# Gated channels one step ahead, four convolution taps a slot, and the context's part of queries and keys first: a change to the first layer of a two-layer trunk

## The chip, the cores and the metric

One core of a Trainium2 chip runs the whole program in one launch. The metric is device time in microseconds; the time before is 1056.01 us, the median of 3 runs (1055.93 to 1057.12). All data is float32. Products are made by TensorE (PE) out of high and low parts: a weight and its rounded copy, and the remainder.

## The reference, cut to what matters

Two layers work on 256 latent tokens (4 rows of 64) and 256 context tokens, 1024 channels wide. In the first layer both streams go through everything; the part that matters here is the token-mixing half:

```
p = h @ w_in[l]                      # columns: GLU | q k v | gates
u = a * sigmoid(g)                   # conv branch: 512 gated channels
u = dwconv1d(u, dw, dw_b)            # depthwise, 31 taps
u = silu(layernorm(u, ln_g, ln_b)) @ w_conv_out
q = rope_2d(q, ...); k = rope_2d(k, ...)           # latent tokens only
s_win = q . k_window * scale + bias; s_ctx = q . k_ctx * scale
p = softmax(concat([s_win, s_ctx]))  # latent queries: window keys and all context keys
y_attn = p_win . v_win + p_ctx . v_ctx             # context queries: context keys only
x = x + g1 * ((sig(gate0) * y_conv + sig(gate1) * y_attn) @ w_out)
```

After it come a gated MLP, and the same again in the second layer.

## The kernel before

**Products.** Activations lie with channels on the partitions. `group` (L201) makes one 128-channel tile of an input projection for 512 tokens (latent and context): 8 channel blocks by 3 matmuls (L197 to L199), 24 matmuls of 128x512, into one of four PSUM banks (tag `main`). Its weights come as one 512 KB tile, `raw`, fetched on SP's queue; ACT rounds it (`whi`, L216) and negates it (`wlo`, L217), and a DMA of POOL's queue (L218) adds `raw` to `wlo`. There are four buffers each of `raw`, `whi` and `wlo`, so that a `whi` is written when PE has done with the one four tiles earlier.

**Slots.** In the middle and at the end of each such group the program passes a `slot()` (L92): each generator in the list `side` goes on by one step. One is the convolution (`conv_run`, L677), which at each slot issues `rate` taps. Another is the attention (`att.run`, L452). The instructions are then put in order for each engine by a scheduler; each engine works its queue in that order.

**Convolution.** `glu(j)` (L687) makes a tile `u` of 128 gated channels out of two groups (ACT takes the gate's tanh, L691; DVE multiplies, L693), and appends 31 taps. A tap is one DVE instruction on 128x512 that adds into the tile `cb` (L671 the first, L673 the other 30). Four tiles make 124 taps. What is left of them when the attention is over is issued by `layer_norm` (L938) with 5 a slot; its sum over the four tiles (L949 to L951) goes to PE in a matmul (L955), after gate group 9.

**Queries and keys.** `qk(j)` (L843), for each of four pairs of heads, makes a group of queries and one of keys. On DVE the latent half is rotated: a product (L859), a shuffle (L860), a product (L861) and a sum (L864 for queries, L869 for keys). Then queries and keys are split into a high part on ACT (L881) and a low part on DVE (L882): the context half in one piece, the latent half of queries in one, that of keys in two of 128x160. In the code these pieces stand after the rotation; keys take the pieces in the order context, first window part, second window part.

**Attention.** `Attention.step` (L457) issues the scores of a pair (L495: 24 matmuls of 64 partitions, of both query tiles and both heads), the softmax (DVE bias and maximum L516, ACT exponential L519, DVE reciprocal L521, ACT scaling L522), the turning of the probabilities on PE (L561, copies on ACT L564) and the products with values (L578, L587). Context queries are done for two pairs at a time (L530 to L540, L567). `ahead(j)` makes steps at once until pair j has been issued.

**The order in the first layer.** The value projection and the first gated tile run first (to 56 us). Then follow `qk(0)`, and for j = 1 to 3 `glu_groups(j)` and `qk(j)`. `rate` is 2.0, and 3 from the end of the first turn of that loop. While the attention has work, up to five gate groups follow (`gate`, L708), and when it is over its memory goes to new tiles, into which modulation rows are loaded (L282, L154) for dot products on DVE (L304). There are 16 gate groups. The values of the window keys go through 16 small DMAs on SP's queue (L728).

Of the kernel before, what the change touches and what calls it, by code (L numbers as in the profile page):

```python
# [19 lines left out]
S = 256  # L20
GW = 64
# [32 lines left out]
def trunk(ctx: ExitStack, tc: tile.TileContext, xt, cvec, crow, wall, wada, params, bias_t, rope_t, out):  # L54
# [13 lines left out]
    def nm(s):  # L68
        uid[0] += 1
        return f"{s}_{uid[0]}"  # L70
# [561 lines left out]
    for l in range(DEPTH):  # L632
# [5 lines left out]
        with ExitStack() if last else start as e1a:  # L638
# [62 lines left out]
            def glu_groups(j):  # L701
                pa = in_group(T_GLU + 2 * (j - 1), ALL)
                pg = in_group(T_GLU + 2 * (j - 1) + 1, ALL)
                copied = None if last else att.ahead(j - 2)
                with tc.issue_after(copied.ins) if copied else ExitStack():
                    glu(j, pa, pg)

# [5 lines left out]
            with ExitStack() as e1b:  # L713
# [126 lines left out]
                rate[0] = 3 if last else 2.0  # L840
                add_side(conv)

                def qk(j):  # L843

                    att.ahead(j - 2)
                    bt = eb.tile([P, 5, NS_ // 2], F32, tag="bias", bufs=2 if last else 1, name=nm("bias"))
                    both = []
                    for what in range(2):
                        w = T if what == 0 else 2 * S
                        sc = HD ** -0.5 if what == 0 else 1.0  # L850
                        ps = in_group((T_Q, T_K)[what] + j, slice(0, w))
                        if what == 0:
                            with tc.issue_after(lastdma[0].ins):
                                sp.dma_start(bt, bias_t[l, j])
                        r1, r2 = tmp(), tmp()
                        got = back(ps[:, :w])
                        lat, ctx_ = (got[:, 0], got[:, 1]) if w > S else (got, None)
                        part = halves if w == S else lambda a: a
                        dve.tensor_tensor(part(r1[:, LAT]), lat, part(rope[:, 0, :]), ALU.mult)  # L859
                        dve.stream_shuffle(part(r2[:, LAT]), lat, SWAP16)  # L860
                        dve.tensor_tensor(r2[:, LAT], r2[:, LAT], rope[:, 1, :], ALU.mult)  # L861
# [8 lines left out]
                        f = eb.tile([P, 2, KN if what else w], F32R, tag="qk"[what], bufs=2, name=nm("qk"))  # L870
                        if what == 0:
                            to = [([f[:, a, LAT] for a in range(2)], rq[:, LAT])]
                            if T > S:
                                to.append(([f[:, a, CTX] for a in range(2)], ctx_))
                        else:
                            rv_ = r1[:, LAT].rearrange("p (r c) -> p r c", r=ROWS)
                            to = [([f[:, a, KCTX] for a in range(2)], ctx_)]
                            for d, c in ((slice(0, KL), slice(GW - TC, GW)), (slice(KX, KN), slice(0, TC))):
                                to.append(([f[:, a, d].rearrange("p (c r) -> p r c", r=ROWS) for a in range(2)], rv_[:, :, c]))
                        for (hi, lo), src in to:  # L880
                            act.activation(hi, src, AF.Identity, scale=sc)  # L881
                            end = dve.scalar_tensor_tensor(lo, src, sc, hi.bitcast(F32), ALU.mult, ALU.subtract)  # L882
                        both.append(f)
                    att.pair(j, *both, bt, end)

                if l == 0:
                    for t in range(4):
                        keep_v(t, pv[t])
                    qk(0)
                    arun = att.run()  # L890
                    add_side(arun)
                    for j in range(1, 4):
                        glu_groups(j)
                        qk(j)
                        rate[0] = 3
                else:
                    glu_groups(2)
                    rate[0] = 3
# [12 lines left out]
                n = 0  # L911
                if last:
                    add_side(arun)
                    for j in range(1, 4):
                        gate(ea, n)
                        n += 1
                        qk(j)
                while att.busy() and n < (14 if last else 5):
                    gate(ea, n)
                    n += 1  # L920
                while att.busy():
# [435 lines left out]
```

## Time and profile before

| | |
|---|---|
| median of 3 runs | 1056.01 us |
| the profiled execution, its own time | 1054.58 us |
| its span | 1052.8 us |
| mean granted TensorE clock | 0.997 |
| PE busy | 1032.4 us (98%) |
| DVE busy | 893.2 us (85%) |
| ACT busy | 565.6 us (54%) |
| first PE matmul of the stage of pairs and gated tiles | 56.20 us |
| matmul of the normalization's sum, L955 | 213.02 us |

A row of the timeline gives the start in the span, the length, engine, line, operation and tile, the count where rows are merged, and in square brackets how long the engine was idle before and who released it. A matmul of 128x512 is shown 0.38 us long, and the next begins 0.216 us later: PE is pipelined, so starts are what counts. The same holds on DVE, where a tap is shown 0.74 to 0.77 us long and the next instruction begins earlier. The waits view sums such idle time by the waiting and the releasing line. The windows view gives, for each stretch, its length, the busy time of the engines with the number of their instructions, the granted clock, the share of the DMA engines and GB/s.

### The profile page before, as it was taken

What the parts mean: (1) busy time and instruction counts of PE and PEld (TensorE: products, weight loads), DVE (VectorE), ACT (ScalarE), POOL (GpSimd) and SP (SyncE); (2) the same over time, 40 slices, a digit from 0 to 9 for tenths busy, and PEclk for the clock granted to TensorE, in tenths of its full rate; (3) what the DMA queues carried; (4) which work ended last, traced back from release to release, by engine and by line L of the source; (5) the groups of instructions that cost most, each with busy time, mean ns of one, the idle gap of its engine ahead of it and who ended that gap; (6) DMA issues with size and microseconds to landing.
All of it is one profiled execution on the core that took longest, in us unless ns stands there. A gap on an engine that the chain in (4) does not pass through costs nothing.

```text
span 1052.8 us, 17991 instructions
## 1 busy us (share of the span) xinstructions
PE 1032.4 (98%) x6886; PEld 932.9 (89%) x6886; DVE 893.2 (85%) x1608; ACT 565.6 (54%) x921; POOL 43.7 (4%) x59
## 2 busy tenths in 40 slices
PE   9999999999999999999999999999999999999997
PEld 7787788888889988888888889999889999999996
DVE  6568899999998787878788888799899988988883
ACT  4458768545434644444444223545777666766652
POOL 1111110011000000000000000000000000000000
PEclk9999999999999999999999999999999999999998
DMA  9989674888945345454545887556734485666781
GB/s 374 305 221 229 156 181 121 258 255 236 305 146 177 104 140 160 140 164 143 166 145 160 301 289 249 180 189 209 208 123 135 161 292 176 193 201 199 221 283 57
DMA packets 59511, 209.26 MB, mean 199 GB/s; under 512 B 7201, under 2 KB 7457, under 8 KB 59425
## 3 DMA queue, kind: packets, MB, share of 16 engines
q1 hardware_dynamic: 54384, 190.77, 55.3%
q0 software_dynamic: 4752, 17.30, 8.7%
q8 instruction: 54, 0.88, 0.3%
q14 instruction: 33, 0.26, 0.1%
q10 hardware_dynamic: 288, 0.04, 0.0%
HBM read 187.63 MB, written 1.05 MB: 179 GB/s over the span
## 4 chain that ended last, share of the span: by engine, by line
PE 68%; DVE 17%; ACT 5%; DMA 4%; issue 3%; SPq 1%; DVEq 0%; ACTq 0%
PE main L197 20%; PE main L198 20%; PE main L199 20%; DVE cb L673 6%; PE main L736 4%; DVE wlo L168 3%; DMA raw<-in_wall 2%; DVE t L304 2%; DMA own<-in_wada 1%; SPq L728 1%; PE sc L197 1%; PE sc L199 1%; PE sc L198 1%; DVE qk L882 1%; ACT pp L519 1%
## 5 line engine op out<-in xcount | busy, mean ns | idle before, releaser
L197 PE MATMUL main<-h,whi 128*128 128x256 f32 (+1 forms) x1328 | 433.1, 326 | 1.2 <-DVE qk L882 1.2
L198 PE MATMUL main<-h,whi 128*128 128x256 f32 (+1 forms) x1328 | 430.2, 324 | 0.9 <-DVE h L1001 0.7
L199 PE MATMUL main<-h,wlo 128*128 128x256 f32 (+1 forms) x1328 | 429.9, 324 | 1.2 <-DVE wlo L168 1.1
L167 ACT CAST whi<-raw 128x1024 fp32r<-128x1024 f32 (+1 forms) x211 | 218.3, 1039 | 234.8 <-PE main L198 173.6
L168 DVE TENSOR_TENSOR wlo<-raw,whi 128x1024 fp32r<-128x1024 f32 (+1 forms) x211 | 253.6, 1208 | 67.2 <-ACT whi L167 66.4
L197 PEld LDWEIGHTS main<-h,whi 128*128 128x128 f32 x1328 | 252.8, 190 | 22.0 <-issue 1.3
L199 PEld LDWEIGHTS main<-h,wlo 128*128 128x128 f32 x1328 | 252.5, 190 | 18.5 <-DVE wlo L168 1.8
L198 PEld LDWEIGHTS main<-h,whi 128*128 128x128 f32 x1328 | 252.7, 190 | 18.3 <-DVE h L1001 1.0
L304 DVE CUSTOM_DVE_ANT_0 t<-own,sb,par 128x1024 bf16<-128x1024 f32 x120 | 151.8, 1282 | 6.8 <-DMA own<-in_wada 6.8
L673 DVE SCALAR_TENSOR_TENSOR cb<-u,par,cb 128x512 f32<-128x512 f32 (+1 forms) x240 | 144.7, 620 | 2.8
L198 PE MATMUL main<-fl,whi 128*128 128x256 f32 (+1 forms) x396 | 122.8, 310 | 0.0
L197 PE MATMUL main<-fh,whi 128*128 128x256 f32 (+1 forms) x396 | 122.8, 310 | 0.0
L199 PE MATMUL main<-fh,wlo 128*128 128x256 f32 (+1 forms) x396 | 122.5, 310 | 0.0
L197 PEld LDWEIGHTS main<-fh,whi 128*128 128x128 f32 x396 | 75.6, 191 | 3.8 <-ACT fh L1095 0.2
L198 PEld LDWEIGHTS main<-fl,whi 128*128 128x128 f32 x396 | 75.6, 191 | 3.7 <-DVE fl L1096 0.2
L199 PEld LDWEIGHTS main<-fh,wlo 128*128 128x128 f32 x396 | 75.5, 191 | 3.6
L216 ACT CAST whi<-raw 128x1024 fp32r<-128x1024 f32 x33 | 34.6, 1049 | 36.0 <-PE main L198 30.5
L404 ACT ACTIVATE h<-t,mod 128x256 fp32r<-128x256 f32 x56 | 25.2, 503 | 34.8 <-DVE t L403 34.3
L218 POOL DMA_DIRECT2D wlo<-raw x33 | 28.9, 877 | 258.9 <-ACT wlo L217 107.6
L736 PE MATMUL main<-whi,h 128*128 128x512 f32 x128 | 38.5, 386 | 0.2
L1105 ACT ACTIVATE t<-t 128x512 f32<-128x512 f32 x22 | 13.9, 632 | 41.3 <-DVE t L1074 41.3
L217 ACT ACTIVATE wlo<-whi 128x1024 fp32r<-128x1024 f32 x33 | 35.0, 1061 | 0.5
(214 smaller groups left out, 1268.8 us busy)
## 6 DMA issues: line engine op xcount, KB each, us to landing
raw<-in_wall SPq DMA_DIRECT2D x240, 512.0 KB, 4.3
own<-in_wada SPq DMA_DIRECT2D x72, 512.0 KB, 4.7
wlo<-raw POOLq DMA_DIRECT2D x33, 512.0 KB, 5.4
raw<-in_wada SPq DMA_DIRECT2D x16, 512.0 KB, 5.8
bias<-in_bias_t SPq DMA_DIRECT2D x8, 520.0 KB, 5.3
row<-in_wada SPq DMA_DIRECT2D x8, 512.0 KB, 5.1
sb<-in_crow SPq DMA_DIRECT2D x5, 512.0 KB, 4.8
x<-in_xt SPq DMA_DIRECT2D x4, 512.0 KB, 5.1
```

The source lines that it names most:

```text
L167: act.copy(hi[:, c], r[:, c])
L168: dve.tensor_tensor(lo[:, c], r[:, c], hi[:, c].bitcast(F32), ALU.subtract)
L197: pe.matmul(ps, w[0], order(xh), start=start, stop=False)
L198: pe.matmul(ps, w[0], order(xl), start=False, stop=False)
L199: pe.matmul(ps, w[1], order(xh), start=False, stop=stop)
L216: act.copy(hi, r)
L217: act.mul(lo, hi.bitcast(F32), -1.0)
L218: pool.dma_start(lo, r, accum_op=ALU.add)
L304: dve.tensor_tensor_reduce(tmp().bitcast(BF16), r, v, 1.0, pr(l, BADA + n, 1), ALU.mult, ALU.add, mods[l][:, n, s : s + 1])
L404: high = act.activation(hi[:, c], y[:, c], AF.Identity, bias=b)
L673: dve.scalar_tensor_tensor(cb[j], src, w, cb[j], ALU.mult, ALU.add)
L736: mm = pe.matmul(pv[t], h1[n == 1][k][:, c], runs(w[n == 2][:, b]), start=k + n == 0, stop=k == KD - 1 and n == 2)
```

## The change

In the first layer `glu_groups(1)` runs ahead of `qk(0)`, and then `glu_groups(j + 1)` ahead of `qk(j)` for j = 1, 2; `qk(3)` comes after the first gate group, and the gate groups that may run while the attention has work are up to eight. `rate` is 4.0 for the whole first layer. In `qk`, for both layers, the split of the context half (in the new helper `parts`) is written ahead of the rotation's second product, and the second window part of the keys ahead of the first. `glu_groups` brings the attention forward to pair j - 3 in place of j - 2.

```
             def glu_groups(j):
...
-                copied = None if last else att.ahead(j - 2)
+                copied = None if last else att.ahead(j - 3)
...
+                def parts(f, d, src, sc, view=lambda a: a):
+                    hi, lo = (view(f[:, a, d]) for a in range(2))
+                    act.activation(hi, src, AF.Identity, scale=sc)
+                    return dve.scalar_tensor_tensor(lo, src, sc, hi.bitcast(F32), ALU.mult, ALU.subtract)
...
                         dve.stream_shuffle(part(r2[:, LAT]), lat, SWAP16)
+                        f = eb.tile([P, 2, KN if what else w], F32R, tag="qk"[what], bufs=2, name=nm("qk"))
+                        if ctx_ is not None:
+                            parts(f, KCTX if what else CTX, ctx_, sc)
...
-                        for (hi, lo), src in to:
-                            act.activation(hi, src, AF.Identity, scale=sc)
-                            end = dve.scalar_tensor_tensor(lo, src, sc, hi.bitcast(F32), ALU.mult, ALU.subtract)
+                            for d, c in ((slice(KX, KN), slice(0, TC)), (slice(0, KL), slice(GW - TC, GW))):
+                                end = parts(f, d, rv_[:, :, c], sc, lambda a: a.rearrange("p (c r) -> p r c", r=ROWS))
...
                 if l == 0:
...
+                    rate[0] = 4.0
+                    glu_groups(1)
                     qk(0)
                     arun = att.run()
                     add_side(arun)
-                    for j in range(1, 4):
-                        glu_groups(j)
+                    for j in range(1, 3):
+                        glu_groups(j + 1)
                         qk(j)
-                        rate[0] = 3
...
-                    for j in range(1, 4):
+                for j in range(1 if last else 3, 4):
+                    if True:
                         gate(ea, n)
                         n += 1
                         qk(j)
-                while att.busy() and n < (14 if last else 5):
+                while att.busy() and n < (14 if last else 8):
```

Two places of the queues show what the scheduler makes of it. The first is DVE's queue in the first layer, between the key projection of pair 1 and the last low part of its keys; `main_943` before and `main_1046` now is the PSUM bank of that key group, `qk_...` the split keys, `cb_...` the tiles into which taps add. Before:

```order
L859 TENSOR_TENSOR t_1012<-main_943,rope_196 128x256
L860 STREAM_SHUFFLE t_1013<-main_943 128x256
L673 SCALAR_TENSOR_TENSOR cb_0_184<-u_0_197,par,cb_0_184 128x512
L861 TENSOR_TENSOR t_1013<-t_1013,rope_196 128x256
L882 SCALAR_TENSOR_TENSOR qk_1018<-main_943,qk_1018 128x256
L869 TENSOR_TENSOR t_1012<-t_1012,t_1013 128x256
L673 SCALAR_TENSOR_TENSOR cb_0_184<-u_0_197,par,cb_0_184 128x512 x2
L882 SCALAR_TENSOR_TENSOR qk_1018<-t_1012,qk_1018 128x4x40 x2
```

The same place now (L864, L865, L869, L877 are the rotation, L846 the low parts):

```order
L865 STREAM_SHUFFLE t_1120<-main_1046 128x256
L673 SCALAR_TENSOR_TENSOR cb_1_185<-u_1_198,par,cb_1_185 128x512
L846 SCALAR_TENSOR_TENSOR qk_1123<-main_1046,qk_1123 128x256
L673 SCALAR_TENSOR_TENSOR cb_1_185<-u_1_198,par,cb_1_185 128x512
L869 TENSOR_TENSOR t_1120<-t_1120,rope_196 128x256
L673 SCALAR_TENSOR_TENSOR cb_1_185<-u_1_198,par,cb_1_185 128x512
L877 TENSOR_TENSOR t_1119<-t_1119,t_1120 128x256
L673 SCALAR_TENSOR_TENSOR cb_1_185<-u_1_198,par,cb_1_185 128x512
L846 SCALAR_TENSOR_TENSOR qk_1123<-t_1119,qk_1123 128x4x40
L673 SCALAR_TENSOR_TENSOR cb_1_185<-u_1_198,par,cb_1_185 128x512
L846 SCALAR_TENSOR_TENSOR qk_1123<-t_1119,qk_1123 128x4x40
```

A tap now stands between each two of these steps, and the context's low part stands ahead of the rotation's second product. From the first `u` (L693) to the last low part of pair 3's keys, DVE's queue holds 72 taps of L673 and 3 of L671 before, and 114 and 4 now; the other instructions of that stretch are the same in number, but for one partial sum more (L953) and one low part of a weight (L168).

The second place is ACT's queue at pair 0. Before, `raw_895` and `raw_944` are weights whose loads stand ahead of the 16 DMAs of L728 on SP's queue:

```order
L216 CAST whi_897<-raw_895 128x1024
L217 ACTIVATE wlo_898<-whi_897 128x1024
L881 ACTIVATE qk_716<-main_672 128x256
L881 ACTIVATE qk_716<-t_714 128x256
L216 CAST whi_946<-raw_944 128x1024
```

Now `raw_902` is the last weight loaded ahead of those 16 DMAs and `raw_994` the first behind them; `qk_800` are the queries of pair 0:

```order
L216 CAST whi_904<-raw_902 128x1024
L691 ACTIVATE t_751<-main_711 128x512
L217 ACTIVATE wlo_905<-whi_904 128x1024
L216 CAST whi_996<-raw_994 128x1024
L217 ACTIVATE wlo_997<-whi_996 128x1024
L845 ACTIVATE qk_800<-main_755 128x256
```

The high part of pair 0's queries now stands behind the rounding of a weight that is loaded after the 16 DMAs. On PE's queue the scores of pair 3 stand behind one gate group before, and behind two now; gate groups 2 to 9 and the normalization's sum follow them in both.

More of the change, by code (lines that the diff above doesn't have):

```diff
@@ L869, in qk @@
                             dve.tensor_tensor(r1[:, LAT], r1[:, LAT], r2[:, LAT], ALU.add)
-                        f = eb.tile([P, 2, KN if what else w], F32R, tag="qk"[what], bufs=2, name=nm("qk"))
                         if what == 0:
-                            to = [([f[:, a, LAT] for a in range(2)], rq[:, LAT])]
-                            if T > S:
-                                to.append(([f[:, a, CTX] for a in range(2)], ctx_))
+                            end = parts(f, LAT, rq[:, LAT], sc)
                         else:
                             rv_ = r1[:, LAT].rearrange("p (r c) -> p r c", r=ROWS)
-                            to = [([f[:, a, KCTX] for a in range(2)], ctx_)]
-                            for d, c in ((slice(0, KL), slice(GW - TC, GW)), (slice(KX, KN), slice(0, TC))):
-                                to.append(([f[:, a, d].rearrange("p (c r) -> p r c", r=ROWS) for a in range(2)], rv_[:, :, c]))
-                        for (hi, lo), src in to:
-                            act.activation(hi, src, AF.Identity, scale=sc)
-                            end = dve.scalar_tensor_tensor(lo, src, sc, hi.bitcast(F32), ALU.mult, ALU.subtract)
+                            for d, c in ((slice(KX, KN), slice(0, TC)), (slice(0, KL), slice(GW - TC, GW))):
+                                end = parts(f, d, rv_[:, :, c], sc, lambda a: a.rearrange("p (c r) -> p r c", r=ROWS))
                         both.append(f)
```

## The prediction

> **What bounds the kernel now.** I read the page first, then the windows of the stages that the change touches, then PE's waits there.
>
> ```profile
> span 1052.8 us, 17991 instructions
> PE 1032.4 (98%) x6886; PEld 932.9 (89%) x6886; DVE 893.2 (85%) x1608; ACT 565.6 (54%) x921; POOL 43.7 (4%) x59
> ```
>
> PE is busy in 98% of the span, so the kernel gains only where PE waits. The profiled execution took 1054.58 us, 1.8 us more than its span, and the median of the runs is 1056.01 us, 1.4 us more again. I sum against the profiled execution and add the difference to the median.
>
> The second window below is cut at the place where the last low part of pair 3's keys is done, the third at the sum of the normalization.
>
> ```profile
> 57.80:153.20 95.40, 91.69 (x576) 77.40 (x576) 83.52 (x187) 68.28 (x132) 13.56 (x16) 1.00 0.80 194
> 153.20:213.00 59.80, 58.65 (x382) 48.55 (x378) 55.58 (x95) 40.35 (x82) 4.37 (x5) 1.00 0.67 195
> 213.00:300.00 87.00, 86.32 (x401) 74.65 (x402) 81.52 (x129) 39.52 (x52) 8.14 (x8) 1.00 0.83 248
> ```
>
> The columns are PE, its weight loads, DVE, ACT, POOL. In the first stretch PE idles 95.40 - 91.69 = 3.7 us and DVE 95.40 - 83.52 = 11.9 us: DVE has some room there, and only that. Later PE idles 1.15 and 0.68 us. Who made PE wait, from 57.8 to 215 us:
>
> ```profile
> PE sc L495 <- ACT pT L567: 1.7, 1, 1.7
> PE po L955 <- DVE ss L951: 1.0, 1, 1.0
> PE sc L495 <- ACT qk L881: 0.9, 1, 0.9
> PE sc L495 <- DVE qk L882: 0.6, 1, 0.6
> PE pt L495 <- ACT pT L564: 0.3, 1, 0.3
> PE pt L561 <- ACT pp L522: 0.3, 1, 0.3
> ```
>
> All of it is 4.8 us, 0.45% of the time, mostly scores waiting for their keys. More than this the change cannot win in these stages, even if it made every wait go away.
>
> **What a step costs.** From PE's timeline come the pace of groups and the end of two scores, from DVE's the pace of taps and of rotation steps, and the ends of the stretch.
>
> ```profile
> 56.20 0.38 PE L197 MATMUL main<-h,whi 128*128 128x512 f32 x1
> ...
> 61.38 0.38 PE L197 MATMUL main<-h,whi 128*128 128x512 f32 x1
> ...
> 94.79 0.38 PE L199 MATMUL main<-h,wlo 128*128 128x512 f32 x1
> ...
> 98.14 0.48 PE L197 MATMUL main<-h,whi 128*128 128x512 f32 x1
> ...
> 104.94 1.08 PE L578 MATMUL po<-pT,V 128*64 128x256 f32 x8
> 106.42 0.94 PE L495 MATMUL sc<-qk,qk 64*128 64x256 f32 x12
> ...
> 154.93 0.44 PE L495 MATMUL pt<-qk,qk 64*128 64x416 f32 x1
> ...
> 155.65 0.48 PE L197 MATMUL main<-h,whi 128*128 128x512 f32 x1
> ```
>
> ```profile
> 57.82 0.69 DVE L693 SCALAR_TENSOR_TENSOR u<-t,sc 128x512 f32<-128x512 f32 x1 [5.05 <-ACT t L691]
> ...
> 62.90 0.74 DVE L673 SCALAR_TENSOR_TENSOR cb<-u,par,cb 128x512 f32<-128x512 f32 x1
> 63.55 0.42 DVE L861 TENSOR_TENSOR t<-t,rope 128x256 f32<-128x256 f32 x1
> 63.89 0.75 DVE L673 SCALAR_TENSOR_TENSOR cb<-u,par,cb 128x512 f32<-128x512 f32 x1
> ...
> 126.91 3.93 DVE L673 SCALAR_TENSOR_TENSOR cb<-u,par,cb 128x512 f32<-128x512 f32 x5
> ...
> 135.65 4.06 DVE L673 SCALAR_TENSOR_TENSOR cb<-u,par,cb 128x512 f32<-128x512 f32 x6
> 139.61 0.69 DVE L693 SCALAR_TENSOR_TENSOR u<-t,main 128x512 f32<-128x512 f32 x1
> ...
> 152.44 0.86 DVE L882 SCALAR_TENSOR_TENSOR qk<-t,qk 128x160 fp32r<-128x160 f32 x2
> 153.18 2.35 DVE L673 SCALAR_TENSOR_TENSOR cb<-u,par,cb 128x512 f32<-128x512 f32 x3
> ```
>
> A group of 24 matmuls takes 61.38 - 56.20 = 5.18 us. A rotation step takes 63.89 - 63.55 = 0.34 us. A tap takes 63.55 - 62.90 = 0.65 us; six taps on alternating tiles take 139.61 - 135.65 = 3.96, 0.66 each; five on one tile 3.93, 0.78 each. I take 0.66, since the new queue puts something else between most taps.
>
> **Four taps a slot and the gated tiles a step ahead** are the change's weight. A slot stands every 12 matmuls, 2.6 us of PE; four taps are 2.64 us of DVE. So at this rate the taps alone fill DVE, and rotation, splits and maxima come on top. The order bears it out: up to pair 3's last keys, DVE's queue holds 114 taps of L673 in place of 72, 4 of L671 in place of 3, one partial sum and one weight's low part more; everything else is the same in number. The last has this row:
>
> ```profile
> L168 DVE TENSOR_TENSOR wlo<-raw,whi 128x1024 fp32r<-128x1024 f32 x2 | 2.4, 1220 | 0.0
> ```
>
> The sum, also of 512 columns, I put at a tap's price. The added work is then 44 x 0.66 = 29.0, and 1.2 for the low part: 30.2 us. With the 83.5 us that DVE worked before, the stretch needs 113.7 us of DVE, where it took 95.4 us of time. The queue is worked in order, and a tap now stands between each two rotation steps, so the keys cannot pass the taps.
>
> **The high part behind a late weight** adds a wait. SP's queue, then ACT's, with ACT's two lengths from the same rows:
>
> ```profile
> 58.21 14.81 SPq L728 DMA_DIRECT2D VW<-t  x16
> 73.53 11.04 SPq L154 DMA_DIRECT2D raw<-in_wall  x5
> ```
>
> ```profile
> 68.59 0.36 ACT L881 ACTIVATE qk<-main 128x256 fp32r<-128x256 f32 x1
> ...
> 77.00 1.05 ACT L216 CAST whi<-raw 128x1024 fp32r<-128x1024 f32 x1 [5.47 <-DMA raw<-in_wall]
> 78.08 1.06 ACT L217 ACTIVATE wlo<-whi 128x1024 fp32r<-128x1024 f32 x1
> ```
>
> The weight behind the 16 small DMAs can be rounded at 77.0 us. Before, nothing urgent stood behind that. Now the high part of pair 0's queries does, and begins at 78.08 + 0.96 = 79.0, done at 79.4. DVE reaches the low part earlier: 57.8 + 0.7 (u) + 14 taps of one tile at 0.78 = 69.4; a second u 0.7, ten alternating taps 6.6 and three rotation steps 1.0 make 77.7. So DVE, and all that is queued behind it (23 taps, pair 0's remaining pieces, then its scores on PE), stands still for 1.7 us. If the small DMAs end sooner, it is nothing.
>
> **The sum.** Pair 3's last low part is ready at 57.8 + 113.7 + 1.7 = 173.2 us in place of 153.2. PE's scores of the second query tile, to the next group, take 155.65 - 154.93 = 0.7 us more: PE goes on at 173.9 in place of 155.65, 18.3 us later. One gate group more is behind it by then, so 5.2 us come off. The wait for L951 (1.0 us) goes too, since the taps are over by about 180 us and the sum is wanted after 220. That leaves 18.3 - 5.2 - 1.0 = 12.1 us. Nothing later gives more back: after 153.2 PE waits only 1.15 + 0.68 us in all, 0.8 without L951's. I take 0.3 of this as gone: **+11.8 us**, 1066.4 us for the profiled execution.
>
> An intermediate point shows the same. Pair 1's scores before began to be wanted at 94.79 + 0.22 = 95.0 and let the next group begin at 98.14. Between the first query product of pair 1 and its last low part the queue held 8 taps, and holds 15 (one of them a first) now: 7 x 0.66 = 4.6 us later, while PE has the value products of pair 0 more to do ahead of them, 106.42 - 104.94 = 1.5 us. So that wait grows by about 3 us; the rest comes at the softmax of pair 1, where taps now stand ahead of and between the maxima, and at pairs 0, 2 and 3.
>
> **The other edits.** Context first saves nothing on the path, since the last low parts follow the rotation either way; it is hidden by the queue of taps, and costs up to one 0.34 us step a piece if that cover is gone. The second window part first lets the first query tile start a piece earlier, but the second tile still ends the scores: 0, at best 0.7 us a pair. Up to eight gates instead of five keep the attention's memory longer, so the dot products begin later. They have 87.00 - 81.52 = 5.5 us of room on DVE from 213 to 300 us; the taps that stood between 153 and 213 are gone, and I put it at 0, at most the 5.2 us of one gate group. The second layer keeps its program but for the order of pieces: 0, within 1 us either way.
>
> **Bounds.** Below: no wait of 1.7, all 0.8 us of later waits gone in place of 0.3, 1 us won in the second layer, and 1 us of overlap that the 83.5 us may count twice: +7.6. Above: DVE's own waits inside the stretch, which I have filled with taps, may stay:
>
> ```profile
> DVE ri L521 <- ACT pp L519: 2.7, 3, 2.3
> DVE ol L596 <- ACT oh L595: 2.1, 1, 2.1
> DVE ri L537 <- ACT pp L535: 1.4, 2, 0.9
> ```
>
> That is 6.2 us: +18.0. I stay below the middle of the two, because taps now stand in front of these reciprocals.
>
> **The rivals.** *Faster:* the added taps fit in DVE's idle time. DVE has 11.9 us, and PE another 5.2 us by its gate group, 17.1 us in all; that decides if what is added costs under 17.1 / 44 = 0.39 us a tap. Then the 4.8 us of waits go: 1056.0 - 4.8 = 1051.2 us. For it speaks that DVE idled 5.05 us ahead of its first u and that most waits above are for keys; against it the 0.66 us of every row of taps.
>
> *No change:* the loss is given back later, since 43 taps no longer stand behind pair 3. For it speaks that DVE worked 55.58 of 59.80 us there; against it that PE, which sets the pace, waits only 1.8 us until 300 us, and its busy 58.65 and 86.32 us are the same matmuls. It would need a lag of at most 5.2 + 1.8 + 2.1 = 9.1 us at pair 3, half of mine, and gives 1054 to 1058 us.
>
> *Slower still, by the clock:* at the end of the span PE works little, and the granted clock (the number behind POOL's, here 1.00, 0.87, 0.50) falls:
>
> ```profile
> 1044.00:1045.00 1.00, 0.61 (x4) 0.52 (x4) 0.33 (x1) 0.42 (x1) 0.00 (x0) 1.00 0.00 0
> 1045.00:1046.00 1.00, 0.39 (x2) 0.21 (x2) 0.17 (x1) 0.26 (x1) 0.00 (x0) 0.87 0.00 0
> 1046.00:1047.00 1.00, 0.21 (x1) 0.00 (x0) 0.75 (x3) 0.00 (x0) 0.00 (x0) 0.50 0.00 0
> ```
>
> Some 2 us of thin work halve it. If PE now waits as long between groups, at pairs 1 and 3, it resumes at half pace. Inside the stretch DVE hides this; behind pair 3's scores it does not. A group at half pace loses 5.2 us at most; half of that, 2.6, gives 1067.8 + 2.6 = 1070.4 us. [...]
>
> **The numbers.** The forecast is 1056.0 + 11.8 = 1067.8 us, with 0.62; the clock 0.22; faster 0.08; no change 0.08. A difference of 0.2%, 2.1 us, is about what a measurement of this kernel can tell. So faster is 0.08, within 0.2% 0.08, slower 0.84. The range goes from the lower bound +7.6 to the upper +18.0, 1063.6 to 1074.0, and holds the clock's case; the other two are the 0.16 left out.
>
> **What would show it.** Right: DVE busy in nearly all of 58 to 175 us; PE waiting at L495 and L561 for DVE and ACT, some 20 us in all; pair 3's scores near 173; the normalization's matmul near 225 rather than 213; the same length from there on. The ACT step shows as a wait of DVE for L845 at 77 to 79 us. Wrong: PE waits under 5 us in the stretch, or DVE idle there above 10 us, or the difference lying behind 230 us.

## The result, and the profile after

The changed kernel takes 1073.53 us, the median of 6 runs (1071.53 to 1079.03), against 1056.26 us for the kernel before (6 runs, 1055.44 to 1057.12). The ratio is 1.0168, with an interval of 1.0143 to 1.0192: 15.1 to 20.3 us slower, by the ratio 17.7, where the forecast was 11.8. 1056.26 x 1.0168 is 1074.0 us, at the very edge of the range and 6.2 us above the forecast of 1067.8. Medians below are of all runs, and ratios leave out the one run at a far lower clock (1328.04 us at 0.752, the kernel with 2.75 taps and the faster pace). The profiled execution took 1071.82 us, 17.2 more than that of before. The page of the changed kernel:

```profile
span 1070.0 us, 17988 instructions
PE 1040.6 (97%) x6886; PEld 937.8 (88%) x6886; DVE 889.4 (83%) x1608; ACT 566.4 (53%) x921; POOL 43.5 (4%) x59
```

The work is the same. PE is shown 8 us busier: matmuls are longer where the granted clock is low (one of 128x512 is shown 0.63 us long at 0.50, around 94 us, and the next begins 0.43 us later; 0.38 and 0.22 us at 1.00), and up to 300 us that took 7.6 us of PE's time (0.0 in the kernel before). The stretch from the first gated tile to the last low part of pair 3's keys, which ended at 153.3 us, now ends at 176.6. First the windows, cut there and at the first dot product; then who made PE and DVE wait inside it, and DVE behind it.

```profile
57.80:176.60 118.80, 106.96 (x614) 88.51 (x613) 112.43 (x232) 74.05 (x141) 14.73 (x17) 0.93 0.70 169
176.60:218.00 41.40, 41.33 (x295) 34.53 (x296) 14.85 (x36) 29.97 (x65) 1.73 (x2) 1.00 0.53 161
218.00:300.00 82.00, 82.00 (x385) 71.54 (x385) 72.75 (x114) 39.92 (x51) 9.88 (x10) 1.00 0.91 271
```

```profile
PE sc L495 <- ACT qk L845: 6.0, 3, 2.6
PE pt L561 <- ACT pp L522: 2.2, 1, 2.2
PE sc L561 <- ACT pp L522: 1.5, 1, 1.5
PE sc L495 <- DVE qk L846: 1.4, 1, 1.4
PE pt L495 <- DVE qk L846: 0.7, 3, 0.2
```

```profile
DVE qk L846 <- ACT qk L845: 2.7, 1, 2.7
DVE ri L521 <- ACT pp L519: 0.9, 2, 0.5
DVE t L864 <- PE main L199: 0.9, 2, 0.5
DVE mx L530 <- PE sc L495: 0.6, 1, 0.6
DVE wlo L168 <- ACT whi L167: 0.2, 1, 0.2
...
DVE ol L596 <- ACT oh L595: 9.5, 4, 5.2
DVE t L304 <- DMA own<-in_wada: 6.8, 1, 6.8
```

Three things are to be seen. DVE works 112.4 of 118.8 us: it sets the pace, as forecast, and PE, idle for 118.80 - 106.96 = 11.8 us in place of 3.7, waits for split keys and for the softmax. ACT's high parts L845 in turn waited for DVE's steps among the taps, in the same stretch:

```profile
ACT qk L845 <- DVE t L865: 4.6, 3, 2.6
ACT qk L845 <- DVE t L872: 4.2, 4, 1.9
...
ACT qk L845 <- DVE t L877: 1.1, 2, 0.6
```

The last row belongs to the high parts that PE waited for. At pairs 0 and 1 ACT stood still for 0.6 us each until the rotation's last step (L877) was done; at pair 2 that step was done at 152.3 us, and ACT was busy for 0.7 us more with a weight (L217). The other two rows are the pieces of context and queries.

And behind the stretch DVE has next to nothing to do: 14.85 of 41.40 us. Its next work, the dot products, waits for rows that go into the memory of the attention: they are asked for from 210.49 us on (186.88 before), as the attention's last results are added up (L596, 210.05 and 210.91 us), and the first dot product begins at 218.14 us (196.55 before).

The lag over the kernel before at the same matmuls shows where the time goes. The next group behind pair 3's scores, and the second sum of squares ahead of the MLP, in the changed kernel:

```profile
177.22 0.48 PE L197 MATMUL main<-h,whi 128*128 128x512 f32 x1
...
353.45 0.50 PE L370 MATMUL pt<-one,ss 128*128 128x1 f32 x4
```

The latter in the kernel before:

```profile
336.37 0.50 PE L370 MATMUL pt<-one,ss 128*128 128x1 f32 x4
```

| place | before | after | lag |
|---|---|---|---|
| next group behind pair 3's scores | 155.65 | 177.22 | 21.6 |
| matmul of the normalization's sum (5.2 us of group work now ahead of pair 3) | 213.02 | 227.8 | 14.8 |
| first sum of squares, L370 | 322.83 | 337.45 | 14.6 |
| second sum of squares, L370 | 336.37 | 353.45 | 17.1 |
| end of the span | 1052.8 | 1070.0 | 17.2 |

So there are two losses: 21.6 less the gate group up to pair 3, of which 1.6 come back by the normalization, and another 2.5 us between 337 and 353 us. The trace names the second. DVE reads each sum of squares (L378) for the normalization behind it, and in the changed kernel dot products stand in front of that step. The changed kernel, then the kernel before:

```profile
339.72 1.28 DVE L304 CUSTOM_DVE_ANT_0 t<-own,sb,par 128x1024 bf16<-128x1024 f32 x1
...
340.93 0.15 DVE L378 TENSOR_SCALAR red<-pt 128x2 f32<-128x2 f32 x1
```

```profile
322.69 1.28 DVE L304 CUSTOM_DVE_ANT_0 t<-own,sb,par 128x1024 bf16<-128x1024 f32 x1
...
323.89 0.16 DVE L378 TENSOR_SCALAR red<-pt 128x2 f32<-128x2 f32 x1
```

The reading begins 340.93 - 337.45 = 3.5 us behind the matmul, in place of 323.89 - 322.83 = 1.1 us. These 2.4 us are as long as the lag's growth, and the same 109 matmuls (80 into `main`, 29 into `sc`) lie between the two sums in both kernels, so it is a loss and not a shift. PE waits 1.6 us in it, where before it waited for nothing; the other 0.9 us are shown as busy time (14.40 in place of 13.54). The dot products began 21.6 us later than before, while PE comes to this place only 14.6 us later.

### The profile page after: what moved, and what is told of

Same layout as the page of the kernel before. It is cut to its first block, busy times and chain, and to the rows that moved or that the text cites. A ratio compares the mean times of both kernels' runs of the same rounds, so it can differ in the third digit from the quotient of the medians.

```text
span 1070.0 us, 17988 instructions
## 1 busy us (share of the span) xinstructions
PE 1040.6 (97%) x6886; PEld 937.8 (88%) x6886; DVE 889.4 (83%) x1608; ACT 566.4 (53%) x921; POOL 43.5 (4%) x59
## 4 chain that ended last, share of the span: by engine, by line
PE 75%; DVE 13%; ACT 4%; DMA 4%; issue 2%; SPq 1%; POOL 0%; DVEq 0%; ACTq 0%; POOLq 0%
PE main L197 22%; PE main L198 22%; PE main L199 22%; DVE cb L673 4%; PE main L736 4%; DMA raw<-in_wall 3%; DVE wlo L168 2%; SPq L728 1%; ACT whi L167 1%; DVE t L304 1%; PE sc L199 1%; DVE qk L846 1%; PE sc L198 1%; PE sc L197 1%; DVE t L403 1%
## 5 line engine op out<-in xcount | busy, mean ns | idle before, releaser
L168 DVE TENSOR_TENSOR wlo<-raw,whi 128x1024 fp32r<-128x1024 f32 (+1 forms) x211 | 252.9, 1204 | 77.9 <-ACT whi L167 74.5
L304 DVE CUSTOM_DVE_ANT_0 t<-own,sb,par 128x1024 bf16<-128x1024 f32 x120 | 150.9, 1277 | 12.3 <-DMA own<-in_wada 12.3
L673 DVE SCALAR_TENSOR_TENSOR cb<-u,par,cb 128x512 f32<-128x512 f32 (+1 forms) x240 | 143.1, 612 | 1.9
L217 ACT ACTIVATE wlo<-whi 128x1024 fp32r<-128x1024 f32 x33 | 35.0, 1060 | 0.5
```

Of the source, the lines that this page charges most:

```text
L168: dve.tensor_tensor(lo[:, c], r[:, c], hi[:, c].bitcast(F32), ALU.subtract)
L217: act.mul(lo, hi.bitcast(F32), -1.0)
L304: dve.tensor_tensor_reduce(tmp().bitcast(BF16), r, v, 1.0, pr(l, BADA + n, 1), ALU.mult, ALU.add, mods[l][:, n, s : s + 1])
L673: dve.scalar_tensor_tensor(cb[j], src, w, cb[j], ALU.mult, ALU.add)
```

## The experiments

Three explanations stood against each other at first. Theory Q: the number of taps in DVE's in-order queue ahead of the keys. Rival O: the order of PE's groups, gated tiles ahead of pairs. Rival W: the late weight's rounding at 77 us, from which the rest follows. Rival C, the clock, came second.

**Three taps a slot, order kept.**

```
-                    rate[0] = 4.0
+                    rate[0] = 3.0
```

> The changed kernel with three taps a slot in place of four in the first layer; the gated tiles stay a step ahead. Up to the last low part of pair 3's keys DVE's queue then holds 95 taps in place of 118. Theory Q (what costs is the number of taps queued on DVE ahead of the keys): 23 x 0.66 = 15.2 us less DVE work ahead of pair 3's scores. The changed kernel resumed PE at 177.2 us where the kernel before did at 155.65, 21.6 us later, 5.2 us of it a gate group; 21.6 - 15.2 = 6.4 us, less 5.2 us for the gate group, leaves +1.2 us, and with the 1 to 2 us lost later in the changed kernel 1056 to 1059 us. The granted clock stays at 1.00 where PE no longer waits 2.5 us. Rival O (the order is at fault: gated tiles ahead of the pairs, whatever the pace of the taps): the order of PE's groups is that of the changed kernel, so 1071 to 1074 us. Rival W (the wait of DVE for ACT behind the late weight, 2.7 us, starts it all): 1070 to 1074 us.

Measured: 1064.33 us (1060.75 to 1068.22), ratio 1.0064 (1.0041 to 1.0087). O and W are out: one number takes most of the loss away, with all groups where they were and the wait at 78 us still there (2.6 us). Q's place is right: pair 3's last low part ends at 162.65 us, 14.0 earlier, where 23 x 0.66 = 15.2 were expected. But Q's time is missed by 5 us. In the profiled run, the longest of its five, PE waited 3.5 us between 296 and 302 us (0.7 in the kernel before, at 292 us) for tiles that ACT and DVE make (L1003, L1004), and DVE was busy without a break from 298 to 306 us. Something behind pair 3 also costs.

**Two and a half taps a slot.** The same line with 2.5.

> The changed kernel with 2.5 taps a slot in the first layer. 78 taps up to pair 3's last low part in place of 118. Theory Q: 40 x 0.66 = 26.4 us less DVE work there, more than the whole lag of 21.6 us, so PE no longer waits for keys behind taps, apart from waits of one instruction's length; the gate group stands ahead for free, and what is lost is at most what PE still waits. 1052 to 1057 us; the taps left over (46 in place of 6) are worked behind pair 3 where PE sets the pace, and the normalization's matmul stands two gate groups later in PE's queue. Rival O: 1071 to 1074 us. Rival B (the taps left over come back behind pair 3, DVE being busy 55.6 of 59.8 us there before): over 1060 us, with PE waiting at the normalization's sum.

Measured: 1062.28 us, ratio 1.0054 (1.0037 to 1.0071). Up to 300 us PE idles 3.0 us, less than the 5.5 of the kernel before, as Q said. The loss is a single wait, from 300 to 345 us:

```profile
PE sc L199 <- DVE wlo L168: 5.4, 1, 5.4
PE po L386 <- POOL rs L380: 0.4, 1, 0.4
PE main L197 <- ACT whi L167: 0.3, 1, 0.3
```

The low part for which PE waits stands in DVE's queue behind eight dot products (L304) that the program issues in one go at the end of the token-mixing half, since they are not done by then: their pace is 0.5 a slot while taps are left, 1.2 after. Neither Q alone nor rival B's place (the normalization) fits. DVE has 78 taps ahead of pair 3 here, about as many as before (75), so these 5.7 us come with the order of groups and the gates at the old pace. I formed theory T: the whole stage up to the MLP is short of DVE. Taps, keys, low parts of weights and dot products share it, and what DVE idles anywhere is missing later.

**Four taps a slot in the kernel before.**

```
-                rate[0] = 3 if last else 2.0
+                rate[0] = 3 if last else 4.0
...
-                        rate[0] = 3
+                        rate[0] = 4.0
```

> The kernel before with four taps a slot in the first layer and nothing else. 109 taps up to pair 3's last low part in place of 75. Theory Q: 34 x 0.66 = 22.4 us more DVE work, of which 11.9 us are DVE's idle time of before; some 5 us of DVE's own waits stay, as in the changed kernel. Pair 3's scores 10 to 16 us later, no gate group ahead to take off, 1 us back at the normalization's sum: 1065 to 1072 us. Rival O: 1055 to 1058 us, since no group moves. Rival W: 1055 to 1058 us, since no weight's rounding stands ahead of pair 0's queries.

Measured: 1066.48 us, ratio 1.0089 (1.0070 to 1.0107), where Q said 1065 to 1072 and O and W no change. PE's waits up to 170 us in it:

```profile
PE pt L495 <- ACT qk L881: 6.4, 2, 4.2
PE pt L561 <- ACT pp L522: 0.8, 2, 0.5
PE pt L495 <- DVE qk L882: 0.7, 1, 0.7
PE pt L495 <- ACT pT L567: 0.4, 1, 0.4
```

The same waits grow from the taps alone, without any group moved.

**The pieces' order alone, in the kernel before.** The new `parts` and its order in `qk`, nothing else.

> The kernel before with the order of pieces of the changed kernel in queries and keys (context's part ahead of the rotation's second product, second window part first), in both layers, and nothing else. Up to pair 3's last low part the same number of taps within one. The prediction put it at 0, at best 0.7 us a pair: 1053.5 to 1057 us, most likely 1056. If the pieces are what makes scores late, 1058 us or more.

Measured: 1057.08 us (12 runs), ratio 1.0001 (0.9988 to 1.0015). No change, as forecast, with the median 0.1 us above the range.

**The small DMAs on ACT's queue.**

```
-                            sp.dma_start(VW[2 * t + r :: ROWS, b], v[at : at + WC])
+                            (sp if last else act).dma_start(VW[2 * t + r :: ROWS, b], v[at : at + WC])
```

> The changed kernel with the 16 small DMAs of the window keys' values on ACT's queue in the first layer in place of SP's. The weights' loads no longer stand behind them, and the high part of pair 0's queries stands ahead of the rounding of later weights on ACT; the number of taps up to pair 3's keys stays 118. In the profile of the changed kernel DVE stood still for 2.73 us at 77.8 us for that high part. Theory Q (DVE's queue with its taps sets the pair's scores, whatever starts it): this stop goes and pair 3's scores come some 2 to 3 us earlier, 1070 to 1072 us. Rival W (the late weight starts all of it): 1056 to 1062 us. If ACT's issuing of 16 DMAs holds its own rounding up instead, 1073 us or more.

Measured: 1074.75 us, ratio 1.0184 (1.0158 to 1.0209), the third case. The edit did not make the stop alone disappear. ACT's queue and then PE:

```profile
60.25 11.57 ACTq L728 DMA_DIRECT2D VW<-t  x16
71.87 0.60 ACT L691 ACTIVATE t<-main 128x512 f32<-128x512 f32 x1 [11.16 <-DMA VW<-t]
```

```profile
PE main L197 <- ACT whi L216: 3.8, 2, 3.6
PE main L199 <- DMA wlo<-raw: 0.7, 1, 0.7
```

The 16 issues held ACT for 11.6 us, weights were rounded late, and PE waited 3.6 us for them. DVE still waited 2.1 us for high parts. How much the 2.7 us stop by itself costs stays open; that it does not start the rest is shown by the runs with fewer taps, which have it too.

**Work in PE's waits, to hold the clock.**

```
+            banks = [[psum(t) for t in tags] for tags in (("sc", "sc"), ("pt", "main"))]
+            if what == LAT and self.l == 0 and its[0][0] < 3:
+                for _ in range(8):
+                    pe.matmul(sl(banks[0][0], 0), ident, ident, start=True, stop=True)
```

> The changed kernel with eight products of 128x128 (the unit matrix by itself, results overwritten) on PE ahead of the scores of each of the pairs 0, 1 and 2, where PE waited 2.5 us and more for the split keys. They add work that fits into these waits and keep PE from standing idle there. Rival C (the granted clock, 0.50 for about 3.4 us after each of these waits, costs what it takes from PE, 1.7 us each, 5.1 us in three): the clock stays at 1.00 after these waits and the time is 1067 to 1070 us. Theory Q (DVE's queue sets the scores, and the slow stretches of PE lie beside it, apart from the 1.5 us that DVE itself waited for PE's results): the clock stays at 1.00 there too, but the waits for keys grow by as much as PE gains: 1071.5 to 1074 us.

Measured: 1073.33 us, ratio 1.0164 (1.0146 to 1.0183), against 1.0168 without. In the changed kernel the clock behind pair 2's wait looks like this; the number behind POOL's is the clock:

```profile
153.00:154.00 1.00, 0.41 (x3) 0.31 (x3) 1.00 (x3) 1.00 (x4) 0.43 (x1) 0.91 0.77 266
154.00:155.00 1.00, 1.00 (x8) 1.00 (x8) 1.00 (x4) 0.04 (x1) 0.43 (x1) 0.50 0.55 221
155.00:156.00 1.00, 1.00 (x7) 0.62 (x4) 1.00 (x4) 0.00 (x0) 0.00 (x0) 0.50 1.05 209
156.00:157.00 1.00, 1.00 (x3) 0.80 (x3) 1.00 (x4) 0.37 (x1) 0.00 (x0) 0.50 1.10 225
157.00:158.00 1.00, 1.00 (x5) 0.83 (x5) 1.00 (x4) 0.53 (x3) 0.00 (x0) 0.89 0.48 86
```

With the filling it stays whole there:

```profile
154.00:155.00 1.00, 0.65 (x4) 0.40 (x6) 1.00 (x4) 0.52 (x3) 0.86 (x1) 1.00 0.80 303
155.00:156.00 1.00, 1.00 (x11) 0.75 (x10) 1.00 (x4) 0.00 (x0) 0.00 (x0) 1.00 0.76 184
156.00:157.00 1.00, 1.00 (x5) 0.89 (x6) 1.00 (x3) 0.00 (x0) 0.00 (x0) 1.00 1.00 201
```

The low stretches behind the waits of pairs 0 and 2 and of pair 1's softmax went; the one behind pair 1's scores stayed, and one came at 178 us behind pair 3. In all, PE time lost to the clock up to 300 us (busy time by what is missing from 1.00, summed over windows of 1 us) fell from 7.6 to 4.4 us, and 6 us of added matmuls found room. Yet pair 3's last low part ended at 177.3 us, not earlier than 176.6, with DVE busy 111.9 us of the same 118.8. In this stretch the clock costs what it takes from an engine that would wait anyway: Q over C. One low stretch stayed, so this run tests 3 of the 7.6 us; for the rest there is only the bound that DVE itself waited for PE's results for no more than 0.9 + 0.6 = 1.5 us in the changed kernel.

**Five gates in place of eight while the attention has work.**

```
-                while att.busy() and n < (14 if last else 8):
+                while att.busy() and n < (14 if last else 5):
```

> The changed kernel with up to five gates in place of eight while the attention has work, as in the kernel before. After pair 3's scores one gate group stands ahead of the turning of its probabilities, in place of one and a half and more, so PE waits for the softmax, some 3 to 5 us and a slow clock after it; but the attention's memory comes free some 10 us earlier, and DVE, which idled 6.8 us for the first modulation rows and some 27 us in all from 183 to 218 us, can begin its dot products earlier. If that idle time of DVE is what costs the 1.6 us of PE's waits near 350 us and the rest behind the normalization, these waits go: 1073 to 1077 us in all, with less lost behind 300 us. If the number of gates does nothing: 1073.5 us.

Measured: 1072.53 us, ratio 1.0155 (1.0140 to 1.0170). That is half a microsecond below what was expected if the gates matter, and within the noise of no change. Two things move against each other. PE waits 1.4 us at 201 us, and in the profiled run the clock took 9.9 us in place of 7.6, so the lag at the second sum of squares is 355.65 - 336.37 = 19.3. But between the two sums of squares lie 14.4 us (from 341.30), where the changed kernel took 16.0 and the kernel before 13.5. DVE worked 35.1 us from 180 to 240 us in place of 28.7, and 7 matmuls more lie between (0.11 us each): the late loss is gone. But this run does not show that the memory was at fault: the rows are asked for only 3.2 us earlier (207.33 us), the first dot product begins 0.6 us earlier (217.56), and PE comes to the first sum of squares 3.9 us later, which by itself gives DVE time to catch up.

**2.75 taps a slot.** The same line with 2.75.

> The changed kernel with 2.75 taps a slot: 85 taps up to pair 3's last low part, between the 78 of 2.5 a slot (1062.3 us) and the 95 of three (1064.3 us). With 2.5 PE waited only 3.0 us up to 300 us, but 5.4 us at 333 us for the low part of a weight that stood behind eight dot products on DVE; with three, DVE idled 10.9 us from 180 to 210 us, and PE waited 2.6 us at pair 2's scores and 3.5 us near 298 us. Theory T (DVE's total work up to the end of the token-mixing half counts: time that it idles anywhere ahead is missing there): no rate gets below the kernel before, 1058 to 1063 us. If only the keys ahead of 180 us counted: 1053 to 1056 us.

Measured: 1063.61 us, ratio 1.0072 (1.0055 to 1.0088): T's end, by half a microsecond above it, and the same wait of 5.4 us behind the dot products at 334 us.

**2.5 taps, and a faster pace of the dot products behind them.**

```
-                    rate[0] = 4.0
+                    rate[0] = 2.5
...
-                    pace[0] = 1.0 if last else 1.2
+                    pace[0] = 1.0 if last else 1.6
```

> The changed kernel with 2.5 taps a slot, and with the pace of the dot products on DVE behind the taps at 1.6 a slot in place of 1.2. With 2.5 taps alone (1062.3 us) PE waited 5.4 us at 333 us for a weight's low part behind dot products that were flushed in one go at the end of the token-mixing half, since the taps had held up the slower pace for longer, and the clock was at 0.5 for 3.4 us behind that wait, 1.7 us more. DVE idled 6.2 us between 210 and 240 us, where the dot products can go. Theory T (only work that DVE can do in its idle time is free): that wait and the slow stretch go, 1062.3 - 7.1 = 1055.2 us, 1053.5 to 1057: no slower than the kernel before, within a few tenths of a per cent. If the dot products only make PE wait at another place, 1058 us or more.

Measured: 1056.71 us (12 runs), ratio 1.0004 (0.9990 to 1.0017). All of the 17 us are gone, with the change's order of groups and pieces and its eight gates still in. In the trace with 2.5 taps alone the clock is at 0.50 for 5.5 us behind the wait (338.4 to 343.8 us), not 3.4, and takes 2.7 us of PE's time, not 1.7. DVE from 180 to 240 us in this kernel (first row), in the changed one, and in the kernel before:

```profile
180.00:240.00 60.00, 60.00 (x331) 51.10 (x330) 58.06 (x93) 31.11 (x51) 4.67 (x5) 1.00 0.76 229
```

```profile
180.00:240.00 60.00, 60.00 (x380) 50.67 (x379) 28.68 (x54) 41.59 (x80) 4.35 (x5) 1.00 0.62 181
```

```profile
180.00:240.00 60.00, 59.03 (x301) 50.17 (x298) 55.38 (x85) 28.83 (x40) 6.41 (x6) 1.00 0.82 251
```

58.1, 28.7 and 55.4 of 60 us: with four taps a slot 40 more taps are done ahead of pair 3's keys, where they stood in the way, and are missing here. Since two constants were changed against the changed kernel (2.5 taps, pace 1.6), the next run takes the pace alone.

**The pace alone, in the kernel before.** The last line of the edit above, as a control.

> The kernel before with the pace of the dot products at 1.6 a slot in place of 1.2, and nothing else: the control for the last kernel. The kernel before flushes two dot products at the end of the token-mixing half and PE waits for nothing there, so nothing is to be won: 1054.5 to 1057.5 us. If the pace by itself wins, it shows here, under 1054 us.

Measured: 1066.33 us, ratio 1.0091 (1.0068 to 1.0113). This I had wrong by 10 us. PE's waits from 200 to 280 us:

```profile
PE main L199 <- DMA wlo<-raw: 4.9, 2, 2.8
PE main L199 <- DVE wlo L168: 1.9, 2, 1.5
PE po L955 <- DVE ss L951: 1.2, 1, 1.2
PE main L197 <- DVE g L993: 0.3, 1, 0.3
```

The kernel before has only 4.6 us of DVE's time to give there. With the faster pace DVE is busy 59.2 of the 60 us from 180 to 240, and the dot products (L304) take 27.0 of the 40 us from 200 to 240 us in place of 20.0, ahead of low parts of weights and of the last taps. Their rows also come on the queue of the weights; how much of the 4.9 us is due to that is not shown. So the pace is a gain only beside the emptier DVE that the change leaves. T does not say this: it counts only what DVE idles, and here a fuller DVE, with other work in front, goes with 10 us more.

**Half of each dot product.**

```
+            cut = slice(0, D // 2 if l == 0 else D)
...
-                    tmp().bitcast(BF16), r, v, 1.0,
+                    tmp().bitcast(BF16)[:, cut], r[:, cut], v[:, cut], 1.0,
```

> The changed kernel with the dot products of the first layer behind the attention worked on half of their columns only (512 of 1024); so their results are those of half a product, and DVE has some 0.6 us less to do in each of the 48 that lie in the token-mixing half, 29 us in all. Theory T: the changed kernel's DVE idles some 27 us from 183 to 218 us, where nothing that it could do is free to run, and lacks them behind; with the dot products halved PE's 1.6 us of waits between 340 and 353 us and what is lost behind go, while nothing changes ahead of the normalization's matmul at 227.8 us: 1069 to 1072 us. If these waits have another cause, they stay: 1073.5 us.

Measured: 1071.06 us, ratio 1.0135 (1.0111 to 1.0159), 3.5 us below the changed kernel by the ratios, whose intervals just overlap. The first sum of squares stands at 337.99 us, the second at 352.52: 14.5 us apart, where the changed kernel took 16.0. DVE reads the first sum at 339.87 us, 1.9 us behind the matmul in place of 3.5, and three dot products, now short ones, still stand in front of it. Five matmuls more than in the changed kernel lie between the two sums here, some 0.5 us. So the late loss follows the length of the dot products: about 2 of the 2.5 us are gone.

**2.75 taps and the faster pace.** Both edits.

> The changed kernel with 2.75 taps a slot and the pace 1.6. With 2.75 taps alone (1063.6 us) PE waited 5.4 us near 337 us, and the clock was at 0.5 for some 5 us. Theory T: these go, 1063.6 - 5.4 - 2.4 = 1055.8 us, 1054 to 1058. If the dot products only make PE wait at another place, 1059 us or more.

Measured: 1057.08 us, ratio 1.0004 (0.9991 to 1.0017). As with 2.5.

The kernels beside each other, from their profiles and runs:

| kernel | taps ahead of pair 3's last low part | it ends at, us | DVE idle 180 to 240 us | ratio |
|---|---|---|---|---|
| before | 75 | 153.3 | 4.6 | 1 |
| 2.5 a slot | 78 | 157.5 | 6.8 | 1.0054 |
| 2.5, pace 1.6 | 78 | 158.1 | 1.9 | 1.0004 |
| 2.75 a slot | 85 | 159.6 | 9.5 | 1.0072 |
| 2.75, pace 1.6 | 85 | 159.6 | 5.6 | 1.0004 |
| three | 95 | 162.7 | 14.7 | 1.0064 |
| before, four | 109 | 164.3 | 22.5 | 1.0089 |
| after (four) | 118 | 176.6 | 31.3 | 1.0168 |
| before, pace 1.6 | 75 | 154.4 | 0.8 | 1.0091 |

In all rows but the three of the kernel before, the end time holds the gate group that stands ahead of pair 3 (5.2 us). With the change's order, PE waits for no split queries or keys up to 85 taps; with 95 it waits 1.4 us for them, with 118 8.1 us. No version beats the kernel before. Five gates together with 2.5 taps, which would part the order of groups from the number of gates, was not run, nor was the faster pace with four taps.

## Where the prediction was wrong, and where it was right

**In short.** The time lies 5.4 us above the forecast, by the profiled executions. Two steps of the sum failed. It put what the dot products lose at 0, since "nothing later gives more back" and freed DVE time was counted as room; measured are 2.6 us lost behind the first sum of squares. And it gave DVE 1.7 us of stops inside the stretch, where 6.4 were measured.

**The direction and the main mechanism were right.** DVE's queue of taps sets the keys, and four taps a slot fill it. The order of pieces cost nothing (ratio 1.0001). The order of groups and the eight gates cost nothing once the dot products go at the faster pace (1.0004), but at the old pace 0.5% stays with 2.5 taps (1.0054), so "at 0" was too simple for them as well. The added taps cost what a tap costs: 112.4 us of DVE work measured in the stretch, 113.7 forecast. The gate group came off, and so did the wait for L951: 1.6 us by the normalization.

**The terms that failed.** First, DVE's own stops. The sum had 1.7 us of them, and the bounds held a further 6.2 that "may stay"; I stayed low because taps stand in front of the reciprocals. Measured are 118.8 - 112.4 = 6.4 us. The reciprocals indeed cost little (0.9 us), but the stop for the late weight was 2.7 in place of 1.7 (its rounding began at 78.05 us in place of 77.00), and three more were not in the list: banks of key groups (0.9), scores (0.6) and a later start (0.4); what is left are pauses too short for the view. With 1.3 us less work and 4.7 more stops, pair 3's last low part came at 176.6 in place of 173.2, 3.4 us late.

Second, and this step failed in kind: "Nothing later gives more back", with 0.3 us of later waits gone, and for the dot products "the taps that stood between 153 and 213 are gone, and I put it at 0". I treated the freed DVE time as room. It is room only for work that may run, and the dot products may not, as long as the attention holds the memory for their rows: DVE idled 31.3 of 60 us and then lacked it. From the first sum of squares on, 2.6 us were lost in place of none. Of these, 2.4 us are the later reading of that sum (L378), behind three dot products; with half dot products about 2 us went. That the memory is what holds the dot products back is read from the times of their loads and from the program; no run tests it alone.

Together: 3.3 more at pair 3's scores, 0.5 more given back by the normalization and the first sum of squares, 2.6 lost behind: 5.4 us, from 11.8 to 17.2.

**Misread rows.** The prediction says that the 4.8 us of PE's waits were "mostly scores waiting for their keys". Only 0.9 + 0.6 = 1.5 us are; 1.7 us name copies of turned probabilities (L567). This lent the faster rival more than the rows give. At pair 1 the trace has 16 taps among the steps where 15 were counted. Neither is in the sum.

**The rivals.** Faster would have needed 0.39 us a tap; a tap still takes 0.66. No change needed a lag of at most 9.1 us at pair 3: it was 21.6, and nothing gave it back. The clock did what the rival said: it fell to 0.50 behind four waits and took 7.6 us of PE time, far more than the 2.6 that I gave it. The waits are of 2.5 to 2.6 us at the scores of pairs 0, 1 and 2 (at pair 0 in three pieces) and of 1.5 us at the softmax of pair 1, where another of 2.2 follows; the low stretches, 3.4, 3.4 and 3.4 us long at the scores and 6.8 at the softmax, begin 0.2 to 1.8 us behind the end of the wait, and after each the clock is at 1.00 again. Yet, as far as the filling tests it, it was not what lengthened this kernel: the forecast's "inside the stretch DVE hides this" held for the 3 us that were won back. Behind pair 3 no low stretch came in the changed kernel (1.00 from 157.3 to 360 us), so the price of 2.6 was not paid. In the last section a wait of 1.7 us was enough.

**The signs named ahead** held in part: DVE was busy in nearly all of the stretch and stood still for L845 until 80.5 us, and the normalization came at 227.8 (near 225 was said). PE's waits did not reach the "some 20 us": 11.8 us were idle, and 7.6 went to the clock. "The same length from there on" failed: 842.2 us in place of 839.8.

## What to carry to other kernels

Work that fills an idle engine must be free to wait: in an in-order queue a filler that stands between the steps of a chain is part of the chain, so its rate has to leave room for the chain at its densest place, not on average. In the kernel before, 109 taps in place of 75 moved the last low part of pair 3's keys from 153.3 to 164.3 us. When work is moved earlier, ask what the engine will do in the place that it leaves; if what comes next there cannot run yet, the time is lost and can be missed later: here DVE idled 31.3 of 60 us, and 2.5 us were lost between 337 and 353 us. And a control in the old kernel is needed for every tuning constant: the pace that repairs this change costs 0.9% without it.

## What the runs showed of the hardware that was not expected

The same wait of PE may or may not cost clock. Up to 180 us the kernel before and the one with the faster pace are the same program. At pair 2's scores both wait 1.7 us, from 127 and from 128 us on. The kernel before:

```profile
127.00:128.00 1.00, 0.00 (x0) 0.00 (x0) 0.96 (x3) 0.98 (x2) 0.00 (x0) 1.00 0.80 176
128.00:129.00 1.00, 0.40 (x1) 0.18 (x1) 0.96 (x2) 1.00 (x4) 0.52 (x1) 1.00 0.95 389
...
131.00:133.00 2.00, 2.00 (x11) 1.76 (x10) 1.78 (x7) 1.23 (x5) 0.00 (x0) 1.00 1.06 262
```

The one with the faster pace:

```profile
128.00:129.00 1.00, 0.00 (x0) 0.00 (x0) 0.96 (x3) 0.99 (x2) 0.00 (x0) 1.00 0.83 242
129.00:130.00 1.00, 0.41 (x1) 0.18 (x1) 0.96 (x2) 1.00 (x4) 0.53 (x1) 1.00 0.79 324
...
131.00:133.00 2.00, 2.00 (x9) 1.33 (x6) 1.96 (x6) 0.50 (x2) 0.00 (x0) 0.50 0.94 256
```

In the second the clock is at 0.50 for some 3.4 us and takes 1.7 us of PE's time; in the first it stays at 1.00. In the changed kernel the four low stretches up to 180 us last 3.4, 3.4, 6.8 and 3.4 us. What decides on which side the same wait falls, no run shows, nor whether runs of one kernel differ for this reason.

Sixteen issues of 64 KB DMAs held ACT's queue for 11.6 us, and took 15.0 us on SP's in the changed kernel: too long for a queue behind which an engine's own work stands, as PE's wait of 3.6 us shows.
